# Rotary embedding and scores on one core: the first batch loaded whole in 16 KB runs, three batches requested ahead of the first store, and worked off in groups of eight heads

## The chip, the cores and the metric

The kernel runs on one core of a Trainium2 chip. A core has several engines that work side by side: TensorE (PE, matrix multiplies and transposes into the accumulation memory PSUM), VectorE (DVE, elementwise work), ScalarE (ACT, here copies out of PSUM), GpSimd (POOL) and SyncE (SP, which here only issues transfers). Each engine works its own list of instructions in order and waits on semaphores for the others. Sixteen DMA engines move data between HBM and the on-chip memory SBUF, which has 128 partitions; a transfer is spread over all sixteen.

The metric is the time of one execution on the device, in microseconds (us). Before the change the median of three runs was 793.49 us, from 793.11 to 793.54.

## The reference: what is computed

q and k have the shape batch 16, sequence 512, heads 16, dimension 64, in fp32. Both get a rotary embedding, and then, for each batch and head, every position of q is multiplied with every position of k:

```python
q1, q2 = q[..., :32], q[..., 32:]
q_rot = concat([q1 * cos - q2 * sin, q1 * sin + q2 * cos], axis=-1)   # k the same
scores = einsum('bshd,bthd->bsht', q_rot, k_rot)                     # fp32
```

q and k are 33.6 MB each, the output is 268.4 MB. So four bytes in five that move are output.

## The kernel before

**Layout.** A batch of q or k is 2 MB (2048 KB, 2.10 million bytes). It is loaded so that partition p holds the four positions 4p to 4p+3 (`c` = 0 to 3), 16 KB in a row in HBM. `G` is 4 heads, `H` 16, `HP` 8 (pairs of heads), `C` 4.

**Steps and pairs.** The work is 64 steps `i`, four to a batch; each step runs eight pairs `p`. `scores(i, p, st)` multiplies one pair of heads (two 64-row products into `ps`, L201) and ACT copies the 128x1024 result into the staging tile `st` (L208). A staging tile holds 16 heads of one `c` (4 MB over all partitions). There are three slots for staging tiles, three buffers for `ps`.

**Rotation.** `rope(which, n)` works on a unit: it returns two closures, `products` (L149 and L150) and `sums` (L154), all on DVE. From batch 1 on, unit `n` is one `c` of a batch with all 16 heads. In batch 0, `n` below 4 is a group of four heads with all `c`, because the first work can then begin when only four heads have been loaded.

**Transposition.** `transposed(which, n, g, copy)` makes PE turn four 128x128 blocks into one PSUM bank (L170), and ACT or DVE copies the bank into `qT` or `kT` (L185). There are two such banks. `tr_act` does both halves `g` of a unit with ACT copies.

**The first batch, before.** The first batch lives in the tile `early`, which takes the third slot of the staging tiles; the tiles of steps 0 and 1 (`st_first`) take the first two. `load_units` (L62) asks for the first four heads of k, the first four of q (512 KB each, runs of 1 KB), then the other twelve of k and of q (1536 KB each, runs of 3 KB). The loads of batch 1 follow at once. Step `i` of batch 0 then does heads 4i to 4i+3 for all four `c`; after every second pair a store of 1024 KB with four heads goes out (L211), 16 in all. The loads of batch 2 are issued by SP at pair 3 of step 0 (k) and of step 1 (q), in SP's list between those stores. The loop writes the order out by hand: DVE closures are kept in a list `dve` and run at pairs 0, 1, 2, 6 and at the end of a step, transpositions at pairs 2 and 6 on ACT, and at pairs 0 and 1 on DVE for the k units of batch 1. `load("k", 3)` follows step 3.

**From step 4 on** (L264) nothing is touched by the change: at pairs 1 and 3 the next q unit is transposed with DVE copies, at pairs 5 and 6 a k unit of the next batch with ACT copies, one 4 MB store goes out per step (L188), and one batch of q and of k is loaded per four steps, each into one of two buffers.

`tc.manual_schedule()` keeps the order as written: each engine's list is the order in which the closures run. SP's list is the order in which transfers are issued, and a store that is not ready holds up what stands behind it on SP.

**Loads with a detour.** Five later loads (`RELIEVED`) go partly over POOL; they are the same in both kernels.

Of the kernel before, what the change touches and what calls it, by code (L numbers as in the profile page):

```python
# [10 lines left out]
def kernel(  # L11
# [8 lines left out]
    nc = tc.nc  # L20
    fp32 = mybir.dt.float32
# [3 lines left out]
    B, S, H, D = q.shape  # L25
    HD = D // 2
    P = 128
    C = S // P
    HP = H // 2
    NST = B * C  # L30
    G = H // C
# [6 lines left out]
    stage_pool = ctx.enter_context(tc.tile_pool(name="stage", bufs=3))  # L38
# [4 lines left out]
    dram = {  # L43
        "q": q.rearrange("b (p c) h d -> b p c h d", c=C),
        "k": k.rearrange("b (p c) h d -> b p c h d", c=C),
    }
    o_v = out.rearrange("b (p c) h t -> b c p h t", c=C)
# [6 lines left out]

    st_first = [stage_pool.tile([P, H, S], fp32, tag="stage", name="st") for _ in range(2)]
    early = stage_pool.tile([P, 2 * C * H * D], fp32, tag="stage", name="early")
    units = {}
    used = [0]  # L60

    def load_units(which, head, heads):  # L62
        n = C * heads * D
        t = early[:, used[0] : used[0] + n].rearrange("p (c e) -> p c e", c=C)
        used[0] += n
        src = dram[which][0, :, :, head : head + heads, :]
        nc.sync.dma_start(t.rearrange("p c (h d) -> p c h d", d=D), src)
        for h in range(0, heads, G):
            units[which, (head + h) // G] = t[:, :, D * h : D * (h + G)]

    batches = {}

# [40 lines left out]
    def load(which, b):  # L113

        if b >= B:
            return
        t = in_pool.tile([P, C, H * D], fp32, tag=which + "_in", name=which + "_sb")
        batches[which, b] = t
        if (which, b) in RELIEVED:
            load_around(which, b, t)  # L120
        else:
            nc.sync.dma_start(t.rearrange("p c (h d) -> p c h d", h=H), dram[which][b])

    def rope(which, n):


        part = part_pool.tile([P, H * D], fp32, tag="part", name="part")
        if n < C:
            x = units[which, n]
            sv, k1, k2 = "p c (g j) -> p c g j", {"j": HD}, {"j": D}  # L130
            cs = cos_t.unsqueeze(2).to_broadcast((P, C, 2 * G, HD))
            ss = ss_v.unsqueeze(2).to_broadcast((P, C, G, D))
            pv = part.rearrange("p (c g j) -> p c g j", c=C, j=D)
            x5 = x.rearrange("p c (h x j) -> p c h x j", x=2, j=HD)
            p5 = part.rearrange("p (c h x j) -> p c h x j", c=C, x=2, j=HD)
            adds = [(x5[:, :, :, y], p5[:, :, :, 1 - y]) for y in range(2)]
        else:
            x = batches[which, n // C][:, n % C]
            sv, k1, k2 = "p (g j) -> p g j", {"j": HD}, {"j": D}
            cs = cos_t[:, n % C].unsqueeze(1).to_broadcast((P, 2 * H, HD))  # L140
            ss = ss_v[:, n % C].unsqueeze(1).to_broadcast((P, H, D))
            pv = part.rearrange(sv, **k2)
            x4 = x.rearrange("p (h x j) -> p h x j", x=2, j=HD)
            swapped = bass.AP(part.tensor, part.offset + HD, [part.ap[0], (D, H), (-HD, 2), (1, HD)])
            adds = [(x4, swapped)]
        xs, xc = x.rearrange(sv, **k2), x.rearrange(sv, **k1)

        def products():
            nc.vector.tensor_tensor(pv, xs, ss, op=mult)  # L149
            nc.vector.tensor_tensor(xc, xc, cs, op=mult)  # L150

        def sums():
            for y, z in adds:
                nc.vector.tensor_tensor(y, y, z, op=add)  # L154

        return [products, sums]

    kT = {}
    qT = {}
# [27 lines left out]
    def store(i, st):  # L187
        nc.sync.dma_start(o_v[i // C, i % C], st)  # L188

    def scores(i, p, st):  # L190

        ps = ps_s_pool.tile([P, 2, S], fp32, tag="ps_s", name="ps")
        b = i // C
        if b == 0:
            c, hp = divmod(p, 2)
            lhs, rhs = qT[i][:, C * hp + c], kT[0][:, 2 * i + hp]
        else:
            lhs, rhs = qT[i][:, p], kT[b][:, p]
        for r in range(2):
            po, rh = ps[:, r, :], rhs[64 * r : 64 * r + 64, :]  # L200
            nc.tensor.matmul(  # L201
                out=po, lhsT=lhs[64 * r : 64 * r + 64, :], rhs=rh, start=True, stop=True
            )
        so, si = st[:, 2 * p : 2 * p + 2, :], ps
        if b > 0:
            so = so.rearrange("s r (t c) -> s r t c", c=C)
            si = si.rearrange("s r (c t) -> s r t c", c=C)
        nc.scalar.copy(out=so, in_=si)  # L208
        if b == 0 and p % 2 == 1:
            c = p // 2  # L210
            nc.sync.dma_start(o_v[0, c, :, G * i : G * (i + 1)], st[:, G * c : G * (c + 1)])  # L211
        elif b > 0 and p == HP - 1:
            store(i, st)

    def tr_act(which, n):
        for g in range(2):
            transposed(which, n, g, nc.scalar.copy)

    def run(ops):
        for op in ops:  # L220
            op()

    with tc.manual_schedule():
        for t, src in ((cos_t, cos), (sin_t, sin)):
            nc.scalar.dma_start(t, src.rearrange("(p c) j -> p c j", c=C))
        for head, heads in ((0, G), (G, H - G)):
            load_units("k", head, heads)
            load_units("q", head, heads)
        load("k", 1)
        load("q", 1)  # L230
        make_identity(nc, ident)
        nc.scalar.copy(out=ss_t[:, :, 0, :], in_=sin_t)
        nc.scalar.mul(ss_t[:, :, 1, :], sin_t, -1.0)
        for which in ("k", "q"):
            run(rope(which, 0))
            tr_act(which, 0)


        for i in range(C):
            st = st_first[i] if i < 2 else stage_pool.tile([P, H, S], fp32, tag="stage", name="st")  # L240
            if i < C - 1:
                dve = rope("k", i + 1) + rope("q", i + 1) + rope("k", C + i)
                nxt = [("k", i + 1), ("q", i + 1)]
            else:
                dve = rope("q", C) + rope("k", C + i) + rope("q", C + 1) + rope("k", 2 * C)
                nxt = [("q", C), ("k", C + i)]
            for p in range(HP):
                scores(i, p, st)
                if p in (0, 1) and i > 0:
                    run(dve[:1])  # L250
                    dve = dve[1:]
                    transposed("k", C + i - 1, p, nc.vector.tensor_copy)
                if p == 3 and i < 2:
                    load("kq"[i], 2)
                if p in (2, 6):
                    m = len(dve) - (4 if p == 2 else 2) - (2 if i == C - 1 else 0)
                    run(dve[:m])
                    dve = dve[m:]
                    tr_act(*nxt.pop(0))
            run(dve)  # L260
        load("k", 3)


        for i in range(C, NST):  # L264
            tr = {}
            if i + 1 < NST:
                tr[1], tr[3] = ("q", i + 1, 0), ("q", i + 1, 1)
            if i + C < NST:
                tr[5], tr[6] = ("k", i + C, 0), ("k", i + C, 1)
            dve = []  # L270
            if i + 2 < NST:
                dve += rope("q", i + 2)
            if i + 1 + C < NST:
                dve += rope("k", i + 1 + C)
            st = stage_pool.tile([P, H, S], fp32, tag="stage", name="st")
            for p in range(HP):
                scores(i, p, st)
                if p not in tr:
                    continue
                if tr[p][0] == "q":  # L280
                    run(dve[:1])
                    dve = dve[1:]
                    transposed(*tr[p], nc.vector.tensor_copy)
                else:
                    transposed(*tr[p], nc.scalar.copy)
            run(dve)
            if i % C == C - 2:
                load("q", i // C + 2)
            elif i % C == C - 1:
                load("k", i // C + 3)  # L290
# [30 lines left out]
```

## Time and profile before

| | |
|---|---|
| median of three runs | 793.49 us |
| span of the profiled execution, first to last instruction | 790.4 us |
| its own time with what lies around the span | not shown apart; the median is 3.1 us above the span |
| bytes moved | 336.18 MB, mean 425 GB/s |
| PE / DVE / ACT busy, share of the span | 87% / 69% / 71% |
| DMA share of the chain that ended last | 49% |
| first store issued by SP | 19.52 us |
| first 4 MB store (step 4) issued by SP | 73.69 us |

A DMA share of 1.0 means that all sixteen engines are busy; a stage table can show a little more, since the packets' times overlap. Busy time is an average over the span, so the first hundred microseconds have to be read apart. "Released by" names what ended a wait.

### The profile page before, as it was taken

The page shows a single profiled execution, that of the slowest core. Times are in us where ns is not written, and L with a number is a line of the kernel's source. Part 1 is how long each engine was busy: PE and PEld are TensorE (multiplying, and loading weights), DVE is VectorE, ACT ScalarE, POOL GpSimd, SP SyncE. Part 2 cuts the span into 40 slices and gives each one's busy share as a digit, 9 for nine tenths or more (in the row PEclk, how much of TensorE's full clock was granted, in tenths as well). Part 3 has the DMA queues.
Part 4 walks back from the last instruction along what each step waited for, and adds up shares of the span by engine and source line. Part 5 has one row for each costly group of instructions (what it writes and reads, how often), then busy time and mean ns, then how long its engine had stood idle before and what let it go on. Part 6 is the DMA issues. An engine that isn't in the chain of part 4 may idle for free.

```text
span 790.4 us, 7750 instructions
## 1 busy us (share of the span) xinstructions
PE 684.4 (87%) x3072; PEld 296.4 (38%) x3072; DVE 544.7 (69%) x516; ACT 562.0 (71%) x647; POOL 11.9 (2%) x24
## 2 busy tenths in 40 slices
PE   4989998988988889798996989889899798799960
PEld 2444443433433334343342433334334343344420
DVE  6999988666766678576785767667678487587400
ACT  3888886865857768486785866777577586588770
POOL 0000000000001000000000001000000000000000
PEclk9999999998999999898998989999899899899995
DMA  9999999999999999999999999999999999999997
GB/s 357 417 425 439 429 430 435 425 435 436 429 429 428 413 432 419 433 423 438 433 427 436 426 432 429 422 432 424 430 432 427 436 429 432 430 432 434 432 429 340
DMA packets 18836, 336.18 MB, mean 425 GB/s; under 512 B 2312, under 2 KB 3592, under 8 KB 4616
## 3 DMA queue, kind: packets, MB, share of 16 engines
q1 hardware_dynamic: 16704, 325.46, 96.4%
q0 software_dynamic: 1808, 10.10, 3.1%
q8 instruction: 24, 0.39, 0.2%
q10 hardware_dynamic: 288, 0.13, 0.1%
q14 instruction: 12, 0.10, 0.0%
HBM read 67.24 MB, written 268.44 MB: 425 GB/s over the span
## 4 chain that ended last, share of the span: by engine, by line
DMA 49%; PE 40%; ACT 5%; DVE 3%; issue 1%; ACTq 0%; SPq 0%; DVEq 0%
DMA out_dram<-st 46%; PE ps L201 30%; PE bank L170 10%; ACT st L208 5%; DMA q_sb<-in_q_dram 2%; DVE part L149 1%; DMA early<-in_k_dram 1%; DVE q_sb L150 0%; DVE k_sb L154 0%; DVE k_sb L150 0%; DVE q_sb L154 0%; DVE early L150 0%; DVE kT_t L185 0%; ACTq L316 0%; DVE early L154 0%
## 5 line engine op out<-in xcount | busy, mean ns | idle before, releaser
L208 ACT COPY st<-ps 128x1024 f32<-128x1024 f32 x512 | 495.7, 1020 | 192.6 <-DMA out_dram<-st 109.8
L201 PE MATMUL ps<-kT_t,qT_t 64*128 64x512 f32 x2048 | 544.0, 649 | 67.0 <-ACT st L208 67.0
L201 PEld LDWEIGHTS ps<-kT_t,qT_t 64*128 64x128 f32 x2048 | 183.6, 196 | 256.2 <-issue 133.3
L185 DVE COPY qT_t<-bank 128x512 f32<-128x512 f32 x118 | 81.6, 691 | 193.9 <-PE bank L170 193.9
L170 PEld LDWEIGHTS bank<-ident,q_sb 128*128 128x128 f32 x480 | 54.2, 149 | 99.0 <-issue 96.4
L170 PEld LDWEIGHTS bank<-ident,k_sb 128*128 128x128 f32 x480 | 50.3, 140 | 96.4 <-DVE k_sb L150 39.5
L170 PE MATMUL bank<-ident,q_sb 128*128 128x128 f32 x480 | 85.1, 304 | 0.9 <-PE ps L201 0.9
L170 PE MATMUL bank<-ident,k_sb 128*128 128x128 f32 x480 | 78.5, 286 | 1.6 <-DVE qT_t L185 1.2
L185 ACT COPY kT_t<-bank 128x512 f32<-128x512 f32 x122 | 72.4, 598 | 6.4 <-PE bank L170 6.4
L154 DVE TENSOR_TENSOR k_sb<-k_sb,part 128x1024 f32<-128x1024 f32 x60 | 73.5, 1225 | 2.1
L150 DVE TENSOR_TENSOR q_sb<-q_sb,cos_t 128x1024 f32<-128x1024 f32 x60 | 73.5, 1225 | 2.1
L150 DVE TENSOR_TENSOR k_sb<-k_sb,cos_t 128x1024 f32<-128x1024 f32 x60 | 73.5, 1225 | 2.0
L149 DVE TENSOR_TENSOR part<-q_sb,ss_t 128x1024 f32<-128x1024 f32 x60 | 73.5, 1225 | 2.0
L149 DVE TENSOR_TENSOR part<-k_sb,ss_t 128x1024 f32<-128x1024 f32 x60 | 73.0, 1216 | 0.9 <-DMA k_sb<-in_k_dram 0.7
L154 DVE TENSOR_TENSOR q_sb<-q_sb,part 128x1024 f32<-128x1024 f32 x60 | 72.9, 1216 | 0.0
L170 PE MATMUL bank<-ident,early 128*128 128x128 f32 x64 | 10.5, 315 | 12.4 <-DVE early L154 10.5
L170 PEld LDWEIGHTS bank<-ident,early 128*128 128x128 f32 x64 | 8.3, 161 | 17.4 <-issue 13.4
L149 DVE TENSOR_TENSOR part<-early,ss_t 128x1024 f32<-128x1024 f32 x8 | 9.8, 1222 | 5.8 <-DMA early<-in_k_dram 5.7
L98 POOL DMA_DIRECT2D q_sb<-in_q_dram x3 | 2.3, 752 | 620.2 <-PE bank L170 446.2
L154 DVE TENSOR_TENSOR early<-early,part 128x512 f32<-128x512 f32 x16 | 10.3, 687 | 0.2
L150 DVE TENSOR_TENSOR early<-early,cos_t 128x1024 f32<-128x1024 f32 x8 | 9.8, 1225 | 0.3
L185 ACT COPY qT_t<-bank 128x512 f32<-128x512 f32 x10 | 5.7, 629 | 3.2 <-PE bank L170 3.2
(12 smaller groups left out, 15.9 us busy)
## 6 DMA issues: line engine op xcount, KB each, us to landing
out_dram<-st SPq DMA_DIRECT2D x60, 4096.0 KB, 24.7
k_sb<-in_k_dram SPq DMA_DIRECT2D x13, 2048.0 KB, 28.3
q_sb<-in_q_dram SPq DMA_DIRECT2D x12, 2048.0 KB, 26.5
out_dram<-st SPq DMA_DIRECT2D x16, 1024.0 KB, 13.8
q_sb<-in_q_dram POOLq DMA_DIRECT2D x3, 1920.0 KB, 27.8
k_sb<-in_k_dram POOLq DMA_DIRECT2D x2, 1920.0 KB, 43.3
early<-in_k_dram SPq DMA_DIRECT2D x1, 1536.0 KB
early<-in_q_dram SPq DMA_DIRECT2D x1, 1536.0 KB
```

Of the source, the lines that this page charges most:

```text
L98: nc.gpsimd.dma_start(dst, src)
L149: nc.vector.tensor_tensor(pv, xs, ss, op=mult)
L150: nc.vector.tensor_tensor(xc, xc, cs, op=mult)
L154: nc.vector.tensor_tensor(y, y, z, op=add)
L170: nc.tensor.transpose(bank[:, x, :], src, ident)
L185: copy(out=dst, in_=src)
L201: nc.tensor.matmul(out=po, lhsT=lhs[64 * r : 64 * r + 64, :], rhs=rh, start=True, stop=True)
L208: nc.scalar.copy(out=so, in_=si)
```

## The change

1. `early` takes the first slot of the staging tiles instead of the third. It is filled by two loads of 2 MB, all heads of k and then all heads of q, in runs of 16 KB. Its views `units[which, n]` are still groups of four heads.
2. The loads of batch 1 and of batch 2 (k, q, k, q) are issued right behind, so six loads stand on SP ahead of the first store.
3. Batch 0 is worked in another order. `order` gives for each step and pair which unit `u` of heads, which `c` and which pair `hp` inside the unit is done. Steps 0 and 1 do units 0 and 1 (eight heads) for `c` 0 and 1, then 2 and 3; steps 2 and 3 do units 2 and 3. A step's staging tile holds two slots `c` of eight heads. A store of eight heads of one `c` (2 MB, runs of 16 KB) goes out after every fourth pair, eight in all.
4. Ahead of the first pair there are now the rotations of k units 0 and 1 and q units 0 and 1, and the transpositions of all of these but q unit 1. A table `plan` names, after which pair of which step, each further rotation (DVE) and transposition (`act` with ACT copies, `dve` with DVE copies) is issued.

```diff
+    early = stage_pool.tile([P, 2 * C * H * D], fp32, tag="stage", name="early")
     st_first = [stage_pool.tile([P, H, S], fp32, tag="stage", name="st") for _ in range(2)]
-    early = stage_pool.tile([P, 2 * C * H * D], fp32, tag="stage", name="early")
...
-    def load_units(which, head, heads):
...
+    def load_units(which, x):
+        t = early[:, x * C * H * D : (x + 1) * C * H * D].rearrange("p (c e) -> p c e", c=C)
+        nc.sync.dma_start(t.rearrange("p c (h d) -> p c h d", d=D), dram[which][0])
+        for n in range(C):
+            units[which, n] = t[:, :, D * G * n : D * G * (n + 1)]
...
+    E8 = 2 * G
+    order = [
+        [(2 * (i // 2) + u, 2 * (i % 2) + c, hp) for c in range(2) for u in range(2) for hp in range(2)]
+        for i in range(C)
+    ]
...
-            c, hp = divmod(p, 2)
-            lhs, rhs = qT[i][:, C * hp + c], kT[0][:, 2 * i + hp]
+            u, c, hp = order[i][p]
+            lhs, rhs = qT[u][:, C * hp + c], kT[0][:, 2 * u + hp]
+            at = E8 * (c % 2) + G * (u % 2) + 2 * hp
...
-        if b == 0 and p % 2 == 1:
-            c = p // 2
-            nc.sync.dma_start(o_v[0, c, :, G * i : G * (i + 1)], st[:, G * c : G * (c + 1)])
+        if b == 0 and u % 2 == 1 and hp == 1:
+            g = i // 2
+            nc.sync.dma_start(
+                o_v[0, c, :, E8 * g : E8 * (g + 1)], st[:, E8 * (c % 2) : E8 * (c % 2 + 1)]
+            )
...
-        for head, heads in ((0, G), (G, H - G)):
-            load_units("k", head, heads)
-            load_units("q", head, heads)
-        load("k", 1)
-        load("q", 1)
+        load_units("k", 0)
+        load_units("q", 1)
+        for b in (1, 2):
+            load("k", b)
+            load("q", b)
...
-        for which in ("k", "q"):
-            run(rope(which, 0))
-            tr_act(which, 0)
+        for which, n in (("k", 0), ("k", 1), ("q", 0)):
+            run(rope(which, n))
+            tr_act(which, n)
+        run(rope("q", 1))
+        plan = {
+            (0, 1): [("act", "q", 1), ("rope", "k", 2), ("rope", "q", 2)],
+            (0, 7): [("rope", "k", 3), ("rope", "q", 3)],
+            (1, 2): [("act", "k", 2)],
+            (1, 5): [("act", "q", 2), ("rope", "k", C), ("rope", "k", C + 1)],
+            (1, 7): [("act", "k", 3), ("act", "q", 3)],
+            (2, 3): [("dve", "k", C, 0)],
+            (2, 4): [("dve", "k", C, 1), ("rope", "k", C + 2)],
+            (2, 6): [("dve", "k", C + 1, 0)],
+            (2, 7): [("dve", "k", C + 1, 1), ("rope", "q", C)],
+            (3, 2): [("dve", "k", C + 2, 0)],
+            (3, 3): [("dve", "k", C + 2, 1), ("rope", "k", C + 3)],
+            (3, 5): [("act", "q", C)],
+            (3, 7): [("act", "k", C + 3), ("rope", "q", C + 1), ("rope", "k", 2 * C)],
+        }
         for i in range(C):
...
             for p in range(HP):
                 scores(i, p, st)
...
+                for what, which, n, *g in plan.get((i, p), ()):
+                    if what == "rope":
+                        run(rope(which, n))
...
+                    elif what == "act":
+                        tr_act(which, n)
+                    else:
+                        transposed(which, n, g[0], nc.vector.tensor_copy)
         load("k", 3)
```

More of the change, by code (lines that the diff above doesn't have):

```diff
@@ L53 @@
     ss_v = ss_t.rearrange("p c x j -> p c (x j)")
+    early = stage_pool.tile([P, 2 * C * H * D], fp32, tag="stage", name="early")
     st_first = [stage_pool.tile([P, H, S], fp32, tag="stage", name="st") for _ in range(2)]
-    early = stage_pool.tile([P, 2 * C * H * D], fp32, tag="stage", name="early")
     units = {}
-    used = [0]
-    def load_units(which, head, heads):
[L63 to L69, printed above, removed]
+    def load_units(which, x):
[3 more added lines that the diff above has]
+            units[which, n] = t[:, :, D * G * n : D * G * (n + 1)]
     batches = {}
@@ L194, in scores @@
         if b == 0:
-            c, hp = divmod(p, 2)
-            lhs, rhs = qT[i][:, C * hp + c], kT[0][:, 2 * i + hp]
+            u, c, hp = order[i][p]
+            lhs, rhs = qT[u][:, C * hp + c], kT[0][:, 2 * u + hp]
+            at = E8 * (c % 2) + G * (u % 2) + 2 * hp
         else:
-            lhs, rhs = qT[i][:, p], kT[b][:, p]
+            lhs, rhs, at = qT[i][:, p], kT[b][:, p], 2 * p
         for r in range(2):
@@ L203, in scores @@
             )
-        so, si = st[:, 2 * p : 2 * p + 2, :], ps
+        so, si = st[:, at : at + 2, :], ps
         if b > 0:
@@ L239 @@
         for i in range(C):
             st = st_first[i] if i < 2 else stage_pool.tile([P, H, S], fp32, tag="stage", name="st")
[L241 to L246, printed above, removed]
             for p in range(HP):
                 scores(i, p, st)
[L249 to L259, printed above, removed]
@@ L260 @@
-            run(dve)
+                for what, which, n, *g in plan.get((i, p), ()):
+                    if what == "rope":
+                        run(rope(which, n))
+                    elif what == "load":
+                        load(which, n)
+                    elif what == "act":
+                        tr_act(which, n)
+                    else:
+                        transposed(which, n, g[0], nc.vector.tensor_copy)
         load("k", 3)
```

## The prediction

> **What bounds the kernel now.** Read first: the row of DMA tenths in the 40 slices of the span, then a table of stages with busy time, clock, DMA share (mean of 16 engines) and GB/s, and the same from 0 to 73.7 us.
>
> ```profile
> DMA  9999999999999999999999999999999999999997
> ```
>
> ```profile
> 2.00:4.00 2.00, 0.00 (x0) 0.00 (x0) 0.00 (x0) 0.91 (x1) 0.39 (x1) 1.00 0.74 207
> 4.00:8.00 4.00, 0.00 (x0) 0.00 (x0) 2.29 (x2) 0.51 (x2) 0.00 (x0) 1.00 1.05 368
> 8.00:20.00 12.00, 8.51 (x35) 5.48 (x36) 11.65 (x14) 4.87 (x7) 0.00 (x0) 1.00 1.03 429
> ...
> 33.00:62.00 29.00, 26.91 (x140) 12.76 (x138) 28.42 (x29) 23.83 (x31) 0.00 (x0) 1.00 1.01 422
> ...
> 73.70:97.00 23.30, 23.30 (x114) 10.17 (x111) 21.88 (x21) 20.12 (x24) 0.00 (x0) 1.00 1.03 441
> ```
>
> ```profile
> 0.00:73.70 73.70, 58.87 (x286) 29.00 (x288) 66.39 (x67) 51.24 (x66) 1.39 (x7) 1.00 0.98 405
> ```
>
> The transfers are full from about 4 us to the end, so the run ends when 336.18 MB have moved; only idle or slow DMA can change the time. But in the first 75 us DVE is full too (28.42 of 29.00 us). So the question is how much work the DMA queue still holds when compute is latest. DVE's first row, the issue order of the queue (SP) and the chain of waits show that place.
>
> ```profile
> 5.67 1.23 DVE L149 TENSOR_TENSOR part<-early,ss_t 128x1024 f32<-128x1024 f32 x1 [5.67 <-DMA early<-in_k_dram]
> ```
>
> ```profile
> 35.18 27.44 SPq L211 DMA_DIRECT2D out_dram<-st  x10
> 62.72 0.57 SPq L122 DMA_DIRECT2D k_sb<-in_k_dram  x1
> 73.69 20.37 SPq L188 DMA_DIRECT2D out_dram<-st  x3
> ```
>
> ```profile
> 68.42 0.69 DVE qT_t L185
> 69.16 0.66 PE bank L170 x4
> ```
>
> By 73.7 us have been requested: cos and sin 0.13 MB, six loads of 2.10 (12.58), sixteen stores of 1.05 (16.78), k of batch 3 (2.10): 31.59 MB. Moved: 405 GB/s x 73.7 us = 29.85 MB. The queue holds 1.74 MB, 4.1 us. The next stores (4.19 MB each; starts 73.7, about 83.7 and 93.7, since the x3 line ends at 94.06) come every 10.0 us. Before the one at 93.7, 39.97 MB are requested; by 97.0, 29.85 + 441 x 23.3 = 40.13 MB have moved: that store's bytes start near 96.6, a lead of only 2.9 us. After it the loads of batch 3 and 4 build a real backlog. So compute may be late by under 3 us here, and the pace in this stretch is PE's, released by the DVE copy at 68.42 (last fence): whatever delays DVE delays these stores.
>
> The rings are not equal: the store issued at 103.74 lands 19.9 us later, at 123.6. It, the q load and the store ahead of it are 10.49 MB, 24.4 us at 430 GB/s; with 1.05 us from last byte to landing (the first k_sb load lands at 19.55, when its 6.42 MB had moved at 18.5) the slowest ring began the 93.7 store at 98.2, not 96.6.
>
> **The change, part by part.**
>
> Loads in 16 KB runs. Removed: two issues and the 1 KB and 3 KB runs that moved at 207 and 368 GB/s from 2 to 8 us. At the 429 of the 16 KB stage behind it the same bytes save 2 x (1 - 207/429) = 1.0 us less 0.1 to 0.3 of latency, and 4 x (1 - 368/429) = 0.6: 1.5 us taken; bounds 0 (the slow start is latency) and 2.
>
> The Trainium skill, "DMA: Bandwidth & Descriptors", Specifications, puts line rate at runs of 512 B and up; by it this saving would be about zero, and the 368 beside 429 GB/s here disagrees.
>
> First data later. DVE's first operation waited for 0.5 MB until 5.67. Now it waits for the whole 2.10 MB of k. SP's first issue starts at 0.74 and its queue's first packets come from 2.0; 2.10 + 0.13 MB at 0.42 is 5.3 us, landing 1.05: 8.4 us. Bounds: 7.9 (0.13 MB aside, 430 GB/s) and 9.9 (the 207 and 368 rows keep their rates). Late by 2.75 us. q lands 4.9 later, when DVE is still on k's second unit; the two batches behind it land by 33, ahead of use.
>
> Under "DMA Optimizations" the skill's page "Perfetto Trace Analysis" says that splitting DMAs may let work start sooner if engines are generally idle. The DMA share here is 1.05, so by its condition unsplitting costs nothing and the forecast would fall by this 2.75; the 5.67 us row says DVE does wait for size.
>
> DVE order. No operation is added: 8 rotations of batch-0 units (each 3.85: 5.67 to 9.52), 7 of later units (3.78), 6 copies; DVE ran them gapless from 5.67 to 66.02, 60.35 us. In the new order k0 k1 q0 q1 k2 q2 k3 q3 and units 4, 5 of k run without needing PE: 8 x 3.85 + 2 x 3.78 = 38.4, so to 46.8. Then DVE must copy unit 4 of k, which PE transposes only after pair 3 of step 2. Where is PE then? q0 is rotated at 8.4 + 11.55 = 19.95; in the trace pair 0's eviction starts 4.06 after that (13.37 to 17.43): 24.0. The q1 transposes and copies (1.1) then stand on the path; pairs 2 and 3 need them: the pair 2 eviction starts at 27.6 and pair 3 ends at 29.6, first 2 MB store. From there ACT takes 0.92 a pair (6.51 us for seven) and 1.1 per transposed unit: pair 7 33.2, second store; k2 in front of pair 3, third store 38.1; q2, fourth 42.9; k3 and q3, 2.2, on ACT with only two banks, then PE four pairs in 3.63: pair 3 of step 2 leaves PE at 48.2, its bank is copied from 48.9 (0.69 after the transposes start, 26.82 to 27.51). DVE idles 2.1 us, and 1.0 more for the second bank, as one pair (1.06) and four transposes (0.58) lie between and its own copy is 0.6. Taken 3.1; bounds 0 (ACT a whole three buffers ahead) and 4.9 (the first rival). Behind the waiting copy DVE has the second copy, the rotation of unit 6 and all that follows; PE waits for them through its two transposition banks.
>
> Sum: DVE is late by 2.75 + 3.1 = 5.9 us at the rotation of unit 8 and at the copy of 68.42, now 74.3; so is PE at 69.16, and the store of 73.7 goes at 79.6, that of 93.7 at 99.6.
>
> Six loads ahead. They are the same 12.6 MB, and SP issues them by 4.9 us (0.66 to 0.70 each) with nothing ready behind; POOL's queue is not touched. What goes is cover: before, loads issued at 22.85 and 33.73 filled DMA between early stores. Now loads end at 2.1 + 12.71/0.427 = 31.9 (33.4 before), and the eight stores of 4.9 us want issuing before 31.9, 36.8, 41.7, 46.5, 51.4, 56.3, 61.2 and 66. They are ready at 29.6, 33.2, 38.1, 42.9, 49.2, 55.0, 60.0 and 65.5: in time until the fifth, then by 1 us, about the start time of a transfer. The k load of batch 3 waits on SP for unit 7's transposes (66.7); only the store of 79.6 is queued behind it. Step 2 writes the slot of the first batch, free when q3 is transposed near 44.6; hidden by ACT, at a microsecond's margin.
>
> Empty queue. All before 79.6 has moved by about 76.2; the store starts after 79.6 plus a start time L. L: 1.3 (0.74 to 2.0, SP's first issue); bounds 0.33 (a store's own issue) and 2.0 (full share only at 3.75). DMA stands 4 to 5 us. The early gain only lengthens that. PE's 10.0 us a step then sets each start until the store of 99.6 + 1.3 = 100.9, which before began at 96.6 on the mean ring and 98.2 on the slowest: +4.3 and +2.7. In the last us the share falls by steps (0.83, 0.76, 0.38 from 782 to 788), so the end is not one ring's alone: nearer the mean, +4.0.
>
> The skill's first page named above, under Latency and other measured facts, gives 0.6 us to the first byte; by it the forecast would be 0.7 less. No gap before shows a restart.
>
> Stores of eight heads. Sixteen 8 KB-run stores become eight with 16 KB runs; 422 against 430 GB/s over 29 us would be 0.5 us, swallowed by the gap. Eight issues of 0.33 fall on SP, which waits 49.5 us there.
>
> The profiled span is 790.4; the median 793.49 lies 3.1 above it, taken as unchanged. 790.4 + 4.0 + 3.1 = **797.5**.
>
> **Rivals.**
>
> Units held apart badly. Units k0 to k3 are interleaved strides of one area. If k1's writes wait for k0's transposes (1.94 us against 1.25), 0.7 is lost, again at q1 behind q0, and some 0.5 where k2's transposes wait for k3's sums. Against: the rotation of q0 wrote at 10.78 while PE read k0 until 11.53, but in another area. Lag 7.7: **799.3**.
>
> No idle on DVE. If PE reaches unit 4 before DVE does, the lag is 2.75 to 3.2: 93.7 + 3.2 + 1.3 - 96.6 = +1.6 on the mean ring, 0 on the slowest: **794.5**, no difference.
>
> Faster. The queue never runs empty: it decides at lag + L under 2.9 (mean ring) to 4.5 (slowest). Then the 1.5 us of the slow start and the 0.5 of longer runs stay: **791.5**. For it: the slow rows at 2 to 8 us are real. Against: first data alone costs 2.75 of lag, with L 4.05.
>
> **How the numbers follow.** Forecast 0.58 (its own range 795.2 to 799.5), units held 0.17, no idle 0.12, faster 0.13. The measurement tells 0.2%, 1.6 us: slower 0.75, same 0.12, faster 0.13. The range 792.3 to 800.8 leaves out most of the faster case and the tail of a late landing (9.9) with held units.
>
> **What would show it.** Right: DVE's first operation near 8.4, DVE idle some 3 us near 47 to 51, last unit-8 rotation near 72, first 4 MB store near 79.6 with a DMA stage below full between 75 and 81, the first slices above 357 GB/s. Wrong: first 4 MB store before 76, DMA share at 1.0 through 85, or a first landing near 6.

## The result, and the profile after

The changed kernel takes 805.45 us (median of five runs, 803.84 to 807.29) against 793.11 for the kernel before on the same chip: a ratio of 1.016, 95% interval 1.0146 to 1.0173. On a second chip it was 804.09 against 793.19, 1.0137 (1.0120 to 1.0154). So it is slower by 11 to 12 us, about three times the 4.0 that was forecast. The profiled execution has a span of 802.1 us, 11.7 more than the span before.

The same table of stages as before the change (stage, its length, busy time and count of PE, PE weight load, DVE, ACT and POOL, granted clock, DMA share, GB/s), now of the changed kernel:

```profile
2.00:4.00 2.00, 0.00 (x0) 0.00 (x0) 0.00 (x0) 0.94 (x1) 0.40 (x1) 1.00 0.57 194
4.00:8.00 4.00, 0.00 (x0) 0.00 (x0) 0.00 (x0) 0.00 (x0) 0.00 (x0) 1.00 0.99 419
8.00:20.00 12.00, 1.71 (x8) 1.57 (x8) 5.48 (x6) 1.09 (x3) 0.00 (x0) 1.00 1.02 433
33.00:62.00 29.00, 28.15 (x146) 13.52 (x144) 25.78 (x27) 25.43 (x31) 0.00 (x0) 1.00 0.87 370
73.70:97.00 23.30, 21.25 (x102) 9.57 (x104) 22.85 (x22) 18.43 (x22) 0.00 (x0) 1.00 0.86 349
```

Between 4 and 8 us the transfers are indeed faster, 419 GB/s instead of 368. But the DMA share, which was 1.0 everywhere, is 0.87 and 0.86 in two later stages. Two stretches are quite empty:

```profile
32.50:36.00 3.50, 3.50 (x18) 1.61 (x20) 3.43 (x4) 2.76 (x4) 0.00 (x0) 1.00 0.00 0
83.50:86.00 2.50, 2.50 (x13) 0.90 (x10) 2.43 (x3) 2.27 (x4) 0.00 (x0) 1.00 0.00 0
```

The first lies between the end of the six loads and the first store, the second ahead of the first 4 MB store. The issue order of SP (start, length, instruction) shows both stores late:

```profile
35.48 35.98 SPq L214 DMA_DIRECT2D out_dram<-st  x8
71.56 0.37 SPq L118 DMA_DIRECT2D k_sb<-in_k_dram  x1
85.31 20.37 SPq L184 DMA_DIRECT2D out_dram<-st  x3
```

The first 4 MB store goes at 85.31, before at 73.69: 11.6 us late, where 5.9 were forecast. DVE's rows say why. Its first instruction, and the two copies before which it sits idle:

```profile
14.38 1.23 DVE L145 TENSOR_TENSOR part<-early,ss_t 128x1024 f32<-128x1024 f32 x1 [14.38 <-ACT ss_t L238]
...
54.36 0.69 DVE L181 COPY kT_t<-bank 128x512 f32<-128x512 f32 x1 [1.68 <-PE bank L166]
56.01 0.69 DVE L181 COPY kT_t<-bank 128x512 f32<-128x512 f32 x1 [0.95 <-PE bank L166]
```

DVE began at 14.38, 8.71 us later than before, and it did not wait for k. It waited for ACT's copy of the sine table, and ACT waited for the table itself. In the chain of work that ended last (start, length, what):

```profile
1.18 12.64 DMA sin_t<-in_sin_dram
13.82 0.02 issue
13.84 0.30 ACT ss_t L237
14.14 0.22 ACT ss_t L238
```

The k load itself had landed at 8.5. It was issued at 0.74, and the list of transfers (after) gives its KB and its us to landing. The 64 KB sine table took until 13.82. Before, it had arrived by 4.9, as ACT's first copy of it shows (second line, before):

```profile
early<-in_k_dram SPq DMA_DIRECT2D x1, 2048.0 KB, 7.8
...
4.92 0.30 ACT L232 COPY ss_t<-sin_t 128x128 f32<-128x128 f32 x1 [2.00 <-DMA sin_t<-in_sin_dram]
```

**Where the 11.7 us are lost.** Three stages of each kernel, first after, then before:

```profile
0.00:100.00 100.00, 73.69 (x358) 36.44 (x360) 81.00 (x81) 63.88 (x79) 1.39 (x7) 1.00 0.91 379
100.00:130.00 30.00, 30.00 (x147) 13.23 (x145) 25.59 (x25) 26.06 (x30) 0.00 (x0) 1.00 0.98 395
130.00:700.00 570.00, 505.22 (x2230) 216.38 (x2228) 397.23 (x372) 405.40 (x465) 10.56 (x17) 0.93 1.00 429
```

```profile
0.00:100.00 100.00, 85.17 (x414) 40.61 (x416) 90.76 (x90) 73.78 (x91) 1.39 (x7) 1.00 0.99 414
100.00:130.00 30.00, 30.00 (x146) 13.23 (x146) 25.60 (x25) 26.11 (x31) 0.00 (x0) 1.00 1.01 432
130.00:700.00 570.00, 505.66 (x2220) 215.46 (x2221) 395.40 (x371) 404.38 (x464) 10.52 (x17) 0.93 1.00 429
```

By 100 us 35 GB/s x 100 us = 3.5 MB are missing, 8.1 us at 430 GB/s. The lateness of 11.6 less the lead of 2.9 would be 8.7. From 100 to 130 us another 1.1 MB, 2.6 us, are lost although the share is full. Over the next 570 us the rate is the same, 429 GB/s. About 1 us is left for the end: the last of the 40 slices, 20 us long, moves 328 GB/s against 340, which is 0.6 us at 430 GB/s.

### The profile page after: what moved, and what is told of

It reads as the page before. It is cut to its first block, busy times and chain, and to the rows that moved or that the text cites. A ratio compares the mean times of both kernels' runs of the same rounds, so it can differ in the third digit from the quotient of the medians.

```text
span 802.1 us, 7727 instructions
## 1 busy us (share of the span) xinstructions
PE 683.2 (85%) x3072; PEld 297.1 (37%) x3072; DVE 544.9 (68%) x516; ACT 561.4 (70%) x647; POOL 12.0 (1%) x24
## 4 chain that ended last, share of the span: by engine, by line
DMA 47%; PE 39%; ACT 7%; DVE 4%; issue 1%; ACTq 0%
DMA out_dram<-st 45%; PE ps L204 29%; PE bank L166 10%; ACT st L211 6%; DMA sin_t<-in_sin_dram 2%; DVE part L145 1%; DVE k_sb L146 0%; DVE k_sb L150 0%; DVE kT_t L181 0%; DVE q_sb L146 0%; DVE early L146 0%; DVE q_sb L150 0%; ACT kT_t L181 0%; DVE early L150 0%; ACT qT_t L181 0%
## 5 line engine op out<-in xcount | busy, mean ns | idle before, releaser
L166 PE MATMUL bank<-ident,early 128*128 128x128 f32 x64 | 11.3, 334 | 23.0 <-DVE early L150 20.2
L150 DVE TENSOR_TENSOR early<-early,part 128x512 f32<-128x512 f32 x16 | 10.4, 688 | 0.3
L237 ACT COPY ss_t<-sin_t 128x128 f32<-128x128 f32 x1 | 0.3, 297 | 10.9 <-DMA sin_t<-in_sin_dram 10.9
```

The costliest lines, as they stand in the source:

```text
L166: nc.tensor.transpose(bank[:, x, :], src, ident)
```

## The experiments

Each run was compared with the kernel before on the same chip (792.5 to 793.2 us there). "Lost by 100" and "lost 100 to 130" are worked out as just shown, from the GB/s of the two stages; lateness is that of the first 4 MB store against 73.69. All columns but the last come from the one profiled execution of each kernel, the last is the difference of medians; the profiled execution on the second chip was one of 806.5 us. The expectations before each result call the two main theories 'late sine' (DVE starts late, and that lateness is what the time is made of) and 'lost cover' (with no loads between the early stores the transfers have gaps).

| run | DVE starts | first 4 MB store | late | lost by 100 | lost 100 to 130 | time less before |
|---|---|---|---|---|---|---|
| the change | 14.38 | 85.31 | 11.6 | 8.1 | 2.6 | +12.3 |
| the change, second chip | 14.41 | 87.74 | 14.1 | 10.5 | 3.0 | +10.9 |
| tables_first | 9.46 | 80.58 | 6.9 | 3.7 | 2.7 | +9.2 |
| tables_first_no_wait | 9.47 | 80.57 | 6.9 | 3.7 | 2.7 | +7.5 |
| small_first | 5.88 | 80.50 | 6.8 | 3.3 | 3.1 | +6.1 |
| small_first_no_wait | 5.71 | 77.23 | 3.5 | 0.7 | 2.2 | +4.3 |
| batch2_between | 14.50 | 90.88 | 17.2 | 15.3 | 1.3 | +17.5 |
| old_order_whole | 9.52 | 79.56 | 5.9 | 4.7 | 0.7 | +5.4 |
| six_ahead_old_order | 5.48 | 77.03 | 3.3 | 0.7 | 2.0 | +2.9 |
| sine_late | 15.37 | 84.24 | 10.6 | 8.8 | 0.8 | +10.4 |
| sine_a_little_late | 7.38 | 75.13 | 1.4 | 0.5 | 0.6 | +1.5 |

Not all of the lateness comes from the edits. In some of the profiled executions the clock granted to PE falls to 0.50 for a few microseconds within the first 100 us. The same two stages of small_first and of tables_first (clock, DMA share and GB/s are the last three columns):

```profile
76.00:78.00 2.00, 2.00 (x8) 1.22 (x8) 1.97 (x3) 1.54 (x2) 0.00 (x0) 0.50 0.58 246
78.00:80.00 2.00, 2.00 (x8) 0.73 (x6) 1.93 (x3) 0.60 (x2) 0.00 (x0) 0.69 0.04 16
...
76.00:78.00 2.00, 1.93 (x10) 0.94 (x11) 2.00 (x3) 0.77 (x2) 0.00 (x0) 1.00 0.79 336
78.00:80.00 2.00, 2.00 (x12) 1.08 (x12) 1.97 (x2) 1.77 (x3) 0.00 (x0) 1.00 0.00 0
```

It happens in the rows of the change on the second chip, small_first, batch2_between and six_ahead_old_order, where the clock from 0 to 100 us is 0.97 or 0.98; in the other rows it is 1.00. In the changed kernel the first 4 MB store follows the k load of batch 3 by 13.75 us in the first profile and by 15.25 on the second chip. So in the first three of these rows, where the stretch lies just ahead of that store, some 1.5 us of the lateness belong to the execution. What lowers the clock is not shown.

### Is it the sine table?

tables_first issues cos and sin on SP, ahead of k, in the changed kernel:

```diff
         for t, src in ((cos_t, cos), (sin_t, sin)):
-            nc.scalar.dma_start(t, src.rearrange("(p c) j -> p c j", c=C))
+            nc.sync.dma_start(t, src.rearrange("(p c) j -> p c j", c=C))
```

> The changed kernel with cos and sin issued on SP ahead of the load of k instead of on ACT's own queue; nothing else. Theory 'late sine': the changed kernel's first rotation waited for the sine table until 14.38 us, because the table's small packets took turns with 16 KB packets, and that lateness of DVE is what the time is made of. Then the first rotation starts near 9.4 us (k landed at 8.5, and two issues more stand ahead of it), the first 4 MB store goes near 80.3 instead of 85.3, and the time falls from 805.5 by about 5 us or a little more, to 798 to 801. Rival 'lost cover': six loads ahead of the first store leave the early stores alone with the compute; the tables don't matter, 803 to 807. Rival 'new order': the order of the units costs the time, 803 to 807.

Measured: 801.93 us, ratio 1.0113 (1.0098 to 1.0128), between the two expected ranges. DVE starts at 9.46, now released by k, and the first 4 MB store goes at 80.58, both within 0.3 us of what was expected.

```profile
9.46 1.23 DVE L145 TENSOR_TENSOR part<-early,ss_t 128x1024 f32<-128x1024 f32 x1 [9.46 <-DMA early<-in_k_dram]
```

Of the 4.7 us gained there 4.4 are still there at 100 us (lost by 100: 3.7 instead of 8.1). The total falls by only 2 to 3 us, short of the 5 expected: this run's last slice moves 291 GB/s instead of 328, which over 20 us is 1.7 us at 430 GB/s. Why the end is slower here stays open. The sine is shown as the cause of DVE's late start; "lost cover" and "new order" as the only cause are refuted, as both said that the tables do not matter.

sine_late does the reverse in the kernel before: only the sine is moved, behind the four loads of the first batch.

```diff
-        for t, src in ((cos_t, cos), (sin_t, sin)):
+        for t, src in ((cos_t, cos),):
...
             load_units("q", head, heads)
+        nc.sync.dma_start(sin_t, sin.rearrange("(p c) j -> p c j", c=C))
```

> The kernel before with one thing changed: the sine table is issued on SP behind the four loads of the first batch, so that it lands near 14 us; loads, order, stores and cover are as before. Theory 'late sine': DVE starts near 14.2 instead of 5.67, the first 4 MB store goes near 82.2 instead of 73.7, and of the 8.5 us of lateness all but some 2.1 (the lead of 2.9 less a start time of 0.8) are seen: 799.5, or up to 802.5 if the transfers are also slower after the gap, as they seem to be in the changed kernel between 110 and 130 us. Rival 'lost cover': with the loads of batch 2 between the stores the lateness is hidden, 793 to 795.

Measured: 803.17 us, 1.0129 (1.0114 to 1.0144). DVE starts at 15.37, 9.7 us late, and the time is 10.4 us longer, 0.7 us beyond the far end of what the first theory gave. One late table costs the old kernel nearly as much as the whole change, although it has loads of batch 2 between its stores. That cover does not hide the lateness: from 24 to 32 us this run's DMA share is only 0.25, since the first of those loads stands on SP behind stores that wait for compute.

### How much lateness is free?

sine_a_little_late moves the sine behind the first two loads only:

```diff
-        for t, src in ((cos_t, cos), (sin_t, sin)):
+        for t, src in ((cos_t, cos),):
...
             load_units("q", head, heads)
+            if head == 0:
+                nc.sync.dma_start(sin_t, sin.rearrange("(p c) j -> p c j", c=C))
```

> The kernel before with the sine table issued on SP behind the first two loads (1 MB), so that DVE starts some 1.7 us later than before and nothing else changes. The lead theory (the queue holds 2.9 us more than compute needs at its tightest point) says that this is hidden: 792.5 to 793.5. Rival 'each microsecond of late compute counts', as sine_late with 10.5 us late and 10.4 us longer could be read: 794.3 to 795.

Measured: 794.42 us, 1.0016 (1.0007 to 1.0025). DVE is 1.7 and the first 4 MB store 1.4 us late, and 1.5 us are paid. By the time the rival is right: the expected free lead did not show. It shows in the bytes: only 0.5 us is missing by 100 us, and 0.6 more between 100 and 130. The rows of the table read so: lost by 100 is the lateness less some 3 with six loads ahead (tables_first 3.7 for 6.9, small_first 3.3 for 6.8, small_first_no_wait 0.7 for 3.5), less 0.9 to 1.9 in the others, and then 0.6 to 3 us go between 100 and 130. So a lead does show in the bytes by 100 us, but what it saves is spent later, and the time comes out near the lateness.

### The parts of the change

**Whole loads alone**, in the old order, with the new `load_units` and with the tables ahead on SP as in tables_first, so that the sine plays no part:

```diff
-        for head, heads in ((0, G), (G, H - G)):
-            load_units("k", head, heads)
-            load_units("q", head, heads)
+        load_units("k", 0)
+        load_units("q", 1)
```

> The kernel before with whole loads of the first batch, and cos and sin ahead of them on SP: old order, small stores, loads of batch 2 between the stores. DVE starts near 9.5, 3.8 us late. The first 4 MB store near 77.5; less the lead of 2.9 and with a start time of 0.8 that is +1.7 us, 794.5, and up to 797 if the transfers also slow down after a gap. Rival 'whole loads are harmless, the new order costs': 792 to 793.5.

Measured: 798.33 us, 1.0065 (1.0051 to 1.0078). That is above both expected ranges. DVE starts at 9.52 and waits another 1.0 for q, the store goes at 79.56, 2 us later than expected, and 5.4 us are paid. Whole first loads with the tables ahead of them on SP cost 5 us by themselves, so the rival 'whole loads are harmless' is refuted.

**Six loads ahead alone**, old order and old small loads:

```diff
-        load("k", 1)
-        load("q", 1)
+        for b in (1, 2):
+            load("k", b)
+            load("q", b)
...
-                if p == 3 and i < 2:
-                    load("kq"[i], 2)
```

> The kernel before with the loads of batch 2 issued ahead of the first store and nothing else: old small first loads, old order, old stores, early in the third slot. 'Lateness of compute is all' says DVE starts at 5.67 and no store is needed earlier than before; what can suffer is the staging slot of step 2, which waits for the stores of step 0 that now queue behind 4 MB more: some 3 to 4 us on ACT near 41, seen in part at the first 4 MB store (near 76), 793 to 796. Rival 'lost cover': a gap in the transfers and 797 or more.

Measured: 796.04 us, 1.0038 (1.0023 to 1.0053). The mechanism was the expected one, and larger. ACT's longest wait, in this run and in the kernel before (who waited for whom, us in total, times, longest):

```profile
ACT st L208 <- DMA out_dram<-st: 7.2, 1, 7.2
...
ACT st L208 <- DMA out_dram<-st: 2.6, 1, 2.6
```

ACT waits 4.6 us longer for step 2's staging slot, where 3 to 4 were expected: the stores that empty it stand behind 4 MB more of loads. ACT's first copy of step 2 starts at 44.75, before at 40.59. Right behind it, from 46 to 50 us, the granted clock is 0.50, so not all that follows is the edit's. The changed kernel has no such wait: its six loads have ended when the first store goes at 35.48, and the second, issued near 39, lands 8.1 us later, ahead of step 2's first copy at 51.26.

**The cover put back** into the changed kernel:

```diff
-        for b in (1, 2):
-            load("k", b)
-            load("q", b)
+        load("k", 1)
+        load("q", 1)
...
+            (0, 3): [("load", "k", 2)],
-            (0, 7): [("rope", "k", 3), ("rope", "q", 3)],
+            (0, 7): [("load", "q", 2), ("rope", "k", 3), ("rope", "q", 3)],
```

> The changed kernel with the loads of batch 2 put back between the early stores (after pairs 3 and 7 of step 0); the sine is late as in the changed kernel. Theory 'late sine': compute is late by the same 11.6 us at the first 4 MB store, the same bytes have to be moved before it, so the time stays, 804 to 807. Rival 'lost cover': DMA has work between the stores again and most of the 12.3 us comes back, 793 to 798.

Measured: 810.27 us, 1.0224 (1.0207 to 1.0241), worse than either expected. 'Lost cover' is refuted as to its sign. The two loads now stand on SP behind stores that are late, at 36.76 and 40.43, and the DMA share is 0.25 from 20 to 30 us, where the changed kernel has 1.00. They also delay the stores: the second, issued at 40.04, lands 15.4 us later (8.1 in the changed kernel), and ACT waits for it, 3.9 us, before its first copy of step 2 at 55.60:

```profile
ACT st L211 <- DMA out_dram<-st: 3.9, 1, 3.9
```

So step 2 writes the slot that step 0's stores empty, in the new order too. That it would take the slot of the first batch, as the order in which the tiles are asked for suggests and the prediction has it, is not what this wait shows.

**Small first loads** in the changed kernel, with the old `load_units` put back and everything else as changed:

```diff
-        load_units("k", 0)
-        load_units("q", 1)
+        for head, heads in ((0, G), (G, H - G)):
+            load_units("k", head, heads)
+            load_units("q", head, heads)
```

> The changed kernel (new order, six loads ahead, stores of eight heads) with the first batch loaded as before: four heads of k, four of q, then twelve of each. The sine's packets then take turns with 1 KB packets and land near 5. 'Late sine and size of the first load' says DVE starts near 5.7, waits only the 2.6 us at unit 4, the first 4 MB store goes near 76.5 and the time is 793.5 to 796. 'New order' or 'lost cover' as the cause: 799 to 806, since both are still in.

Measured: 799.00 us, 1.0079 (1.0065 to 1.0092). That is above the range of the first theory and at the lower edge of the rivals'. DVE starts at 5.88, so first data and the sine together are worth 5 to 6 us. But 6 remain, more than expected. DVE's waits add up to 1.3 (for the twelve heads of k, at 11.0) and 3.5 (before the copies of unit 4 of k), 5.0 with the 0.2 at the start; the store is 6.8 late, and PE's last twelve matmuls ahead of it, at 77.36, take 3.76 us where they took 2.85 in tables_first, which is the stretch of low clock shown above. Six loads ahead alone cost 2.9 us, so the new order with its larger stores would be some 3 of the 6.1; this is a difference of two runs, as the new order was not run without the six loads.

**DVE's idle time.** tables_first_no_wait, on top of tables_first, moves the rotation of unit 6 ahead:

```diff
-            (1, 5): [("act", "q", 2), ("rope", "k", C), ("rope", "k", C + 1)],
+            (1, 5): [("act", "q", 2), ("rope", "k", C), ("rope", "k", C + 1), ("rope", "k", C + 2)],
...
-            (2, 4): [("dve", "k", C, 1), ("rope", "k", C + 2)],
+            (2, 4): [("dve", "k", C, 1)],
```

> As tables_first, and the rotation of unit 6 of k is run right behind units 4 and 5 (step 1, pair 5) instead of after the copies of unit 4, so DVE has work while PE comes to unit 4. Theory 'late sine, then the idle of DVE': the 2.6 us that DVE waits before the copies of unit 4 go away too, the first 4 MB store goes near 77.7, the time is 796 to 798.5. 'Lost cover' and 'new order': no better than tables_first by more than 1 us.

Measured: 800.24 us, 1.0096 (1.0079 to 1.0113), but the store still goes at 80.57. The wait had only moved to the copies of the next unit:

```profile
54.32 0.69 DVE L181 COPY kT_t<-bank 128x512 f32<-128x512 f32 x1 [1.57 <-PE bank L166]
55.96 0.69 DVE L181 COPY kT_t<-bank 128x512 f32<-128x512 f32 x1 [0.95 <-PE bank L166]
```

The edit did not do what it was for. The 1.7 us less than tables_first are not the store's: the last slice moves 322 GB/s here and 291 there, 1.4 us at 430 GB/s. small_first_no_wait spreads the work further: on top of small_first, the same move of unit 6, and

```diff
-            (2, 4): [("dve", "k", C, 1), ("rope", "k", C + 2)],
+            (2, 4): [("dve", "k", C, 1), ("rope", "q", C)],
...
-            (2, 7): [("dve", "k", C + 1, 1), ("rope", "q", C)],
+            (2, 7): [("dve", "k", C + 1, 1)],
```

> As small_first, and DVE given work for its idle time: unit 6 of k is rotated behind units 4 and 5, and unit 4 of q between the copies of units 4 and 5 of k (moving unit 6 alone only moved the wait, of 2.5 us, to the copies of unit 5). Expected by the theory that lateness of compute is all: the first 4 MB store near 74 to 75, no gap in the transfers after the first stores, 791.5 to 793.5, as the kernel before or a little better, as the stores of the first batch move 16 KB at a time. 'New order' or 'lost cover': not below 797.

Measured: 797.22 us, 1.0048 (1.0035 to 1.0060), store at 77.23. It is the best of the kernels with the new order, and yet 4.3 us longer than before, not level; by the time the rival holds (not below 797). The edit did only part of what it was for: DVE still waits 1.3 us for the twelve heads of k and 1.8 before its copies, and the store is 3.5 us late instead of the expected 0.3 to 1.3. There is hardly a gap any more (0.7 us lost by 100); 2.2 us are lost between 100 and 130.

### The loss between 100 and 130 us

The last column but one of the table divides cleanly: the seven rows of the six kernels with six loads ahead of the first store (the change on both chips, tables_first, tables_first_no_wait, small_first, small_first_no_wait, six_ahead_old_order) lose 2.0 to 3.1 us there, at shares of 0.97 to 1.00, the four with batch 2 between the stores 0.6 to 1.3. In this stretch q of batch 3 and k of batch 4 are loaded (in the changed kernel issued at 105.78 and 115.80), with the six ahead the first loads since 32 us but for one of k. An idea was that the 16 rings, having run dry together, switch from stores to loads at one moment. In the changed kernel stages of half a microsecond alternate:

```profile
91.00:91.50 0.50, 0.50 (x6) 0.33 (x6) 0.50 (x1) 0.50 (x2) 0.00 (x0) 1.00 2.43 1049
91.50:92.00 0.50, 0.50 (x3) 0.27 (x4) 0.50 (x1) 0.50 (x2) 0.00 (x0) 1.00 0.00 0
```

1049 GB/s over 0.5 us is 0.52 MB, sixteen packets of 32 KB: they start within the one stage, and none in the next, as if each ring had started one. Four kernels tried to tell, and with the first of them the change itself ran once more, without an edit:

> The changed kernel as it is, beside the next run on the same chip: 804 to 807.

Measured: 804.09 us.

staggered adds a tiny load into an unused tile `scrap`, behind the store of step 4:

```diff
+    scrap = const_pool.tile([P, 64], fp32, name="scrap")
...
             if i == C:
+                src = bass.AP(q.tensor, 0, [(512, 8), (2, 40), (1, 1)])
+                nc.sync.dma_start(scrap[:8, :40].rearrange("p (a b) -> p a b", b=1), src)
```

> The changed kernel and one tiny transfer more: behind the first 4 MB store SP issues a load of 40 separate elements into 8 partitions of an unused tile, which puts half of the 16 rings some 0.4 us behind the others. In the changed kernel all rings start that store at one moment after a dry queue and stay in step, and between 110 and 130 us it moves less at a full share. Theory 'loads in step are slow': out of step the loads of batch 3 are not stretched, about 2 us come back, 802.5 to 804.5. Rival 'the loss between 110 and 130 has nothing to do with step': no change, or up to 0.5 us longer.

Measured: 806.00 us, 1.0164 (1.0148 to 1.0179), 400 GB/s from 100 to 130, where the change had 395 and 389. staggered_more is the same with 120 elements at `i == C + 2`:

> The changed kernel and one tiny transfer, now 120 elements and placed right in front of the load of q of batch 3, where the queue does not run dry afterwards: eight rings begin that load about 1 us after the others. (With 40 elements behind the first 4 MB store the offset was about 0.3 us and was lost again before the load.) Theory 'loads in step are slow': between 115 and 125 us, where the changed kernel moves 305 to 351 GB/s, it moves 390 or more, and the time is 803 to 805, as the eight rings carry 1 us more. Rival 'no matter of step': 305 to 351 GB/s again and 804.5 to 807.

Measured: 808.11 us, 1.0186 (1.0169 to 1.0203), 371 GB/s. SP's issue of the q load behind the 120 elements took 10.26 us instead of 0.37, so this run tells nothing of step.

staggered_store uses a store instead, to a place that is written again later; small_first_no_wait_staggered adds the same lines to small_first_no_wait:

```diff
             if i == C + 2:
+                nc.sync.dma_start(o_v[B - 1, C - 1, :8, :12], st[:8, :12])
```

> The changed kernel and one more store: behind the 4 MB store of step 6 eight partitions of twelve heads (24 KB each) go once more, to a place of the last batch that its own store overwrites later. Eight rings are then some 0.9 us behind the other eight, when the load of q of batch 3 and the k load after it move. 'Loads in step are slow': between 100 and 130 us it moves 415 GB/s or more instead of 395, the time falls by 1 to 2 us, to 803 to 804.5. 'Step doesn't matter': 390 to 400 GB/s, 804 to 807.

Measured: 808.18 us, 1.0178 (1.0164 to 1.0192), 380 GB/s.

> small_first_no_wait with the same additional store. It was 4.3 us longer than the kernel before, and between 107 and 117 us it moved 333 GB/s. 'Loads in step are slow': 390 or more there, and 795 to 796.2 instead of 797.2. 'Step doesn't matter': 333 again, 796.5 to 798.5.

Measured: 799.04 us, 1.0073 (1.0060 to 1.0085), 383 GB/s from 100 to 130 and 301 from 107 to 117, where it was 333.

All four took longer than both of their expected ranges: none of the additions brought time back, and each cost some of its own. Behind the additional store, for one, SP's issue of the next k load took 3.0 to 3.1 us instead of 0.6, and the profiles of staggered_more and staggered_store have the low clock. Step is not supported, and not excluded either: the profile does not say to which ring a packet belongs, so it is not shown that half of the rings were set back. What is shown is only the grouping: the loss goes with three batches ahead of the first store, in the old order (six_ahead_old_order, 2.0) as in the new, and it halves where batch 2 is put back (batch2_between, 1.3). Its mechanism stays open.

## Why the prediction was wrong

Direction and chain were right, the size was not.

**"First data later" failed.** It put DVE's first operation at 8.4, from the landing of k, and k did land at 8.5. But the operation reads the sine table too, and the step counted the tables only as 0.13 MB that take their bytes' time. The sine took 12.64 us to landing. The term was 2.75 and measured 8.71. The trace before held the hint: its sine landed at 4.9, in front of k by 0.7 only, while its neighbours on the other queue were 1 KB packets. tables_first and sine_late show both directions. The term is 5.96 us too small, and the forecast's 4.0 fell 7.7 short of the 11.7 of the spans. How much of the 7.7 is this step's alone is less sharp: issuing the tables first took 4.7 us off the store's lateness and 2 to 3 us off the time, as the end of that run was slower.

**"DVE order" held:** an idle time of 3.1 was forecast before the two copies, near 47 to 51; it was 1.68 + 0.95 = 2.6, at 54. The sum of both terms, 11.3, is the store's 11.6.

**"Empty queue" was right in place, not in size.** A lead of 2.9 less a start time of 1.3, so 1.6, was to be taken off the lateness; the 8.1 us lost by 100 are 3.5 less than the lateness of 11.6. The start time was taken too long: the store issued at 85.31 has its first packets in the half microsecond from 86.0, 0.7 to 1.2. The rest of the difference was not resolved.

**A term was missing:** the 2.6 us between 100 and 130. "Six loads ahead" was costed at nothing but lost cover. Loads put back between the late stores brought nothing, as batch2_between showed, but having none there was not free. The same step has step 2 write the slot of the first batch; the wait in batch2_between shows step 0's slot. In the changed kernel this cost nothing, as the stores of step 0 had landed in time.

**"Loads in 16 KB runs" was partly right:** 419 for 368 GB/s between 4 and 8 us, but the stage from 2 to 4 us stayed slow (194 GB/s, 207 before), so its slowness is a start and not the runs. The gain was swallowed, as forecast.

**"790.4 + 3.1"** mixed two things: in each run the time lies 1.7 to 1.8 us above its own span; the profile before was of a run near 792.1.

The rival "units held apart badly" did not happen: DVE ran without waits from 14.38 to 52.7, and k1's writes began at 19.49 while PE transposed k0 until 20.2. "No idle" is refuted by DVE's waits of 1.68 and 0.95 us, "faster" by the two empty stretches.

The profile after shows what made the sine late. Packets, MB and share of SP's queue (q1) and of the tables' own (q10) in the stages 4 to 6, 8 to 10 and 12 to 14 us, after:

```profile
q1 hardware_dynamic: 50, 0.82, 95.5%
q10 hardware_dynamic: 49, 0.03, 4.1%
...
q1 hardware_dynamic: 60, 0.87, 101.4%
q10 hardware_dynamic: 59, 0.03, 4.5%
...
q1 hardware_dynamic: 65, 0.80, 94.0%
q10 hardware_dynamic: 48, 0.02, 3.1%
```

While the tables last, one table packet goes for each 16 KB packet, 49 beside 50 and 59 beside 60. The tables have 288 packets, 18 to an engine; 18 turns at 16 KB x 16 / 430 GB/s = 0.61 us are 11 us. From 2 us that is 13, where their packets ended. The 288 packets also stand in the queue list of the profile before, so this estimate could have been made there.

The Trainium skill, "DMA: Bandwidth & Descriptors", section Queues, rings and completion order, has the rule: an engine takes turns between the queues that have work for it, a packet at a time. The trace agrees with the turns, but the page gives a packet as typically 9 to 17 descriptors, and here each turn was a single 16 KB run.

## What to carry to other kernels

An operation starts when the last of its inputs lands, the small ones too: a small table on a queue of its own is not ahead of the large loads but takes turns with their packets, so enlarging the packets delays it. Issue such tables on the same queue ahead of the large loads, or check what else the first instruction reads before costing a larger first load. And a transfer-bound kernel whose compute is full at its start has no time to give there: here every kernel that made the first 4 MB store later by 1.4 to 17 us was longer by as much to within 1 us, whichever part of the change did it, but for tables_first (9.2 for 6.9) and the change on the second chip (10.9 for 14.1 by the median, 13.3 in the execution that was profiled).

## What the runs showed of the hardware that was not expected

- A 64 KB table had 12.64 us to landing beside 16 KB packets, and 3.7 beside 1 KB packets (the list of transfers before).
- A stage can be full and slow: 395 GB/s at a share of 0.98 from 100 to 130 us, where the kernel before moves 432 at 1.01.
- Behind a transfer of 8 x 120 single elements, the issue of an ordinary 2 MB load took 10.26 us instead of 0.37. Why is not shown.
- The granted clock can fall to 0.50 for a few microseconds in one execution and not in another: with it the twelve matmuls ahead of the first 4 MB store took 3.76 us (small_first), without it 2.85 (tables_first).
